# The fourth and fifth half-size products of a pair change places

## The chip, the cores and the metric

The kernel runs on one core of a Trainium2 chip. The metric is the device time of one execution in microseconds (us). A trace of one profiled execution stands beside the times. In it PE is TensorE's matmuls and PEld its weight loads, DVE is VectorE, ACT is ScalarE, POOL is GpSimd, SP is SyncE, which here only issues transfers; a name with a q is an engine's instruction queue issuing something.

## The reference

One layer of a state-space mixer over a sequence of 512 tokens with width 2048, all in float32:

```python
def reference(x, ...):                     # x: (1, 512, 2048)
    hn = rmsnorm(x, ln_g)
    proj = hn @ w_in                       # 2048 x 10304: z 4096 | x, B, C 6144 | dt 64
    xbc = silu(causal_depthwise_conv(xbc, conv_w, conv_b))
    dt = softplus(dt + dt_bias)
    y = ssd_chunked_scan(xs * dt, dt * a, bm, cm) + d_skip * xs    # 64 heads of 64, state 128
    y = rmsnorm(y * silu(z), norm_g)
    x = x + y @ w_out                      # 4096 x 2048
    return rmsnorm(x, final_g)
```

## The kernel before

**Precision.** A float32 operand is split into a high part (a cast to fp32r by ScalarE, line 87) and a low part (the difference, by VectorE, line 88). A product then takes three matmuls: high by high, high by low, low by high.

**Tiles.** The 80 tiles of 128 columns of the input projection are worked off in twos: a tile of x with one of z (32 of these), a tile of B with one of C (8). The first four twos are multiplied plainly. The other 36 go through `pair`, which uses a fast scheme with seven half-size products in place of eight. The weights of the two tiles, each in two halves of the contraction, are the blocks R11, R12 (first half of the contraction, first and second tile), R21, R22 (second half). Out of them come sums: T1 = R11 + R12, T2 = T1 + R22, T3 = R12 + R22, T4 = T2 + R21. (Signs are taken up by the forms of the activations, which are made ahead.) The output projection uses the same scheme in `opair`, in two groups of four pairs, between plain stretches.

**One pair of the input projection.** Each product is 24 matmuls of 128 x 128 by 256 (8 blocks of the contraction by 3). There are three accumulators in PSUM: S (half of one of two banks that take turns), R (one bank, used by every pair) and A (a bank). With a pair ahead of it, a pair runs, in TensorE's order:

1. R11 into S, then ScalarE copies S to A (line 651)
2. T1 into R, then ScalarE copies R out to `sn[:, 1]` (line 656)
3. T4 of the pair before into that pair's A
4. R22, on top of T1, into R
5. T2, on top of R11, into S, then ScalarE copies S out to `sn[:, 0]` (line 670) and VectorE adds R to it (line 671)
6. R21 into A
7. T3, on top of R11 and T2, into S, from which lines 675 and 676 read

The first pair has no pair ahead of it; it starts with T1, then R11, and lets its third place free.

**Preparing the weights.** Each of the R blocks is a transfer of 512 KB. `q_load` issues it on SP (line 81) into the raw buffers `ra` (three, for R11), `rb` (one, for R12) and `rc` (two, for R22 and R21 in turn). `q_fetch` lets POOL add a block to a raw buffer in place by an accumulating transfer (line 598: T1 and T3). `q_add` adds in place on VectorE (line 604: T2 on top of T1's raw piece, and T4 on top of T2's). `q_split` makes the high and low parts: R11 has a pair of buffers of its own, `h1h` and `h1l`, and all the others take turns in three pairs, `hi` and `lo`.

**Order.** The program order of TensorE, SP and POOL is the order in which the kernel is written. Work around the products is entered as events at a step: a pair is 28 steps long, a product four, and `run(step)` emits what is due. `q_events` enters a pair's loads, sums and splits by an offset to the pair's first step b. ScalarE and VectorE are ordered by a planner when the kernel is built: program order is their priority, `urgent()` raises it, and the planner's model of durations decides when something counts as ready. Between the products the scan's work for the tiles done before (transposes, decay, state, gate) is emitted in the same way. With each pair of B and C comes the convolution of these two tiles.

In the output projection S and R take turns in six banks, and VectorE reads them into the accumulator in SBUF: line 881 reads R after T1, line 893 R after R22, line 896 S after T2, line 898 A, line 903 S after T3; line 902 is ScalarE's copy for the last product. Its splits are urgent.

Of the kernel before, what the change touches and what calls it, by code (L numbers as in the profile page):

```python
# [13 lines left out]
ALU = mybir.AluOpType  # L14
# [6 lines left out]
KT = DM // P  # L21
# [13 lines left out]
def mamba_layer(ctx: ExitStack, tc: tile.TileContext, d: dict, out: bass.AP):  # L35
    nc = tc.nc
    V, S, T, Q = nc.vector, nc.scalar, nc.tensor, nc.gpsimd
# [3 lines left out]
    urgent = tc.high_priority  # L41
# [67 lines left out]
    NPL = 8  # L109
# [6 lines left out]
    quads = seq[NPL // 2:]  # L116
    tile_of = {"z": 0, "x": 32, "B": 64, "C": 72}
    QS = 28
# [21 lines left out]
    base = [END]  # L140
# [77 lines left out]
    q0, q1 = slice(0, 4), slice(4, 8)  # L218
# [203 lines left out]
    def g_c(g):  # L422
        gr[g]["C"] = conv_silu(40 + g, "bc")
        gr[g]["Cs"] = split(gr[g]["C"][:, LH:L], [P, LH], "cst", 2)
# [182 lines left out]
    qs = {}  # L607
    oquads = [blk for blk in blocks if type(blk) is tuple]

    def q_events(n, b, last, e=0, t1=0):  # L610
        for o, f, a in ((-38 - e, q_load, ("R11", 0, 0, "ra")), (-23 - e, q_split, ("R11", True)),
                        (-23 - e, q_fetch, ("T1", "R11", 0, 1)), (-3 - e // 2 - t1, q_split, ("T1",)),
                        (-12 - e // 2, q_load, ("R22", 1, 1, "rc")), (1 - e // 2, q_add, ("T2", "T1", "R22")),
                        (5, q_split, ("R22",)), (9, q_split, ("T2",)),
                        (-8, q_load, ("R21", 1, 0, "rc")), (12, q_add, ("T4", "T2", "R21")),
                        (13, q_split, ("R21",)),
                        (-7, q_load, ("R12", 0, 1, "rb")), (-7, q_fetch, ("T3", "R12", 1, 1)),
                        (17, q_split, ("T3",)), (23 if last else 29, q_split, ("T4",))):
            add(b + o, f, n, *a)
# [7 lines left out]
    def product(ps, w, f, first, step):  # L627

        for k in range(KH):
            if k % 2 == 0:  # L630
                run(step + k // 2)
            hi, lo = w()
            ah, al = operand(f, k)
            T.matmul(ps, hi[:, k, :], ah, start=first and k == 0, stop=False, skip_group_check=True)  # L634
            T.matmul(ps, hi[:, k, :], al, start=False, stop=False, skip_group_check=True)  # L635
            T.matmul(ps, lo[:, k, :], ah, start=False, stop=k == KH - 1, skip_group_check=True)  # L636

    def pair(n, prev):

        b = NPL * KT + n * QS  # L640
        (kp, ip), (kq, iq) = quads[n]
        s_, r_ = ps_s.tile([P, L], F32, name="S")[:, lo_], ps_q.tile([P, LH], F32, name="R")
        sn = sp.tile([P, 2, LH], F32, name="sn")
        zq = xr[:, 3:L + 3] if kq == "C" else sp.tile([P, L], F32, name="z", bufs=2)
        W = lambda f: lambda: qs[n, f]
        A = ps_mm.tile([P, L], F32, name="mm")

        def first(step):
            product(s_, W("R11"), 11, True, step)
            with urgent():  # L650
                S.copy(out=A[:, lo_], in_=s_)

        def second(step):
            product(r_, W("T1"), 1, True, step)
            with urgent():
                S.copy(out=sn[:, 1, :], in_=r_)  # L656

        if prev:
            first(b)
            second(b + 4)  # L660
            prev(b + 8)
        else:
            second(b)
            first(b + 4)
            for i in range(8, 12):
                run(b + i)
        product(r_, W("R22"), 4, False, b + 12)
        product(s_, W("T2"), 2, False, b + 16)
        with urgent():
            S.copy(out=sn[:, 0, :], in_=s_)  # L670
            V.tensor_tensor(out=zq[:, lo_], in0=r_, in1=sn[:, 0, :], op=ALU.add)
        product(A[:, lo_], W("R21"), 12, False, b + 20)
        product(s_, W("T3"), 3, False, b + 24)
        with urgent():
            V.tensor_tensor(out=zq[:, hi_], in0=s_, in1=sn[:, 1, :], op=ALU.add)
            S.copy(out=A[:, hi_], in_=s_)  # L676
        if kq == "C":
            V.scalar_tensor_tensor(out=zq, in0=zq, scalar=-1.0, in1=rbc, op0=ALU.mult, op1=ALU.mult)
            g_c(iq)
        else:  # L680
            V.tensor_tensor(out=zq, in0=zq, in1=rbc, op=ALU.mult)
            S.activation(zq, zq, AF.Silu, scale=-1.0)
            un[iq]["z"] = zq

        def last(step):
            product(A[:, hi_], W("T4"), 22, False, step)
            with urgent():
                normed(A)
            (g_b if kp == "B" else u_x)(ip)
            qs.pop(n)  # L690
        return last
# [4 lines left out]
    def add(step, f, *a):  # L696
        ev.setdefault(step, []).append((f, a))
# [8 lines left out]
        for o, f in zip(w, (u_load, u_decay, u_xt, u_state, u_yd, u_yo)):  # L706
            add(at["x", u] + o, f, u)
    for n in range(len(quads)):
        q_events(n, NPL * KT + n * QS, n == len(quads) - 1, 0 if n else 14)
    for i in range(4):  # L710
        add(49 + 7 * i, x_forms, i // 2, i % 2)
        add(114 + 4 * i, x_form3, i)
# [1 line left out]
    def run(step):  # L714
        for f, a in ev.pop(step, ()):
            f(*a)
# [80 lines left out]
    prev = None  # L797
    for n in range(len(quads)):
        prev = pair(n, prev)


    step = END
# [46 lines left out]
    def oproduct(ps, i, w, f, first, step):  # L849

        yh, yl = yform[i, f]
        for t in range(2):
            tt = slice(t * P, (t + 1) * P)
            for k in range(4):
                if k % 2 == 0:
                    run(step + 2 * t + k // 2)
                hi, lo = w()
                st, en = first and t == 0 and k == 0, k == 3
                T.matmul(ps[:, t, :], yh[:, k, tt], hi[:, k, :], start=st, stop=False, skip_group_check=True)  # L859
                T.matmul(ps[:, t, :], yl[:, k, tt], hi[:, k, :], start=False, stop=False, skip_group_check=True)  # L860
                T.matmul(ps[:, t, :], yh[:, k, tt], lo[:, k, :], start=False, stop=en, skip_group_check=True)  # L861

    def opair(i, s, b, prev):

        n = len(quads) + 4 * i + s
        s_, r_ = [ps_o.tile([P, 2, LH], F32, name="mm") for _ in range(2)]
        W = lambda f: lambda: qs[n, f]
        c = [slice(s * L + h * LH, s * L + h * LH + LH) for h in range(2)]
        p0, p1 = acc[:, 0:2, c[0]], acc[:, 2:4, c[0]]
        q0, q1 = acc[:, 0:2, c[1]], acc[:, 2:4, c[1]]  # L870
        A0 = ps_mm.tile([P, 2, LH], F32, name="mm")

        def first(step):
            oproduct(s_, i, W("R11"), 11, True, step)
            with urgent():
                S.copy(out=A0, in_=s_)

        def second(step):
            oproduct(r_, i, W("T1"), 1, True, step)
            with urgent():  # L880
                V.tensor_tensor(out=q1, in0=q1, in1=r_, op=ALU.subtract)

        if prev:
            first(b)
            second(b + 4)
            prev(b + 8)
        else:
            second(b)
            first(b + 4)
            for k in range(8, 12):  # L890
                run(b + k)
        oproduct(r_, i, W("R22"), 4, False, b + 12)
        V.tensor_tensor(out=q0, in0=q0, in1=r_, op=ALU.subtract)
        oproduct(s_, i, W("T2"), 2, False, b + 16)
        with urgent():
            V.tensor_tensor(out=q0, in0=q0, in1=s_, op=ALU.subtract)
        oproduct(A0, i, W("R21"), 12, False, b + 20)
        V.tensor_tensor(out=p0, in0=p0, in1=A0, op=ALU.add)
        oproduct(s_, i, W("T3"), 3, False, b + 24)
        A1 = ps_mm.tile([P, 2, LH], F32, name="mm")  # L900
        with urgent():
            S.copy(out=A1, in_=s_)
        V.tensor_tensor(out=q1, in0=q1, in1=s_, op=ALU.subtract)

        def last(step):
            oproduct(A1, i, W("T4"), 22, False, step)
            V.tensor_tensor(out=p1, in0=p1, in1=A1, op=ALU.add)
            qs.pop(n)
        return last
# [38 lines left out]
    m = 0  # L948
    for i, blk in enumerate(blocks):
        if type(blk) is tuple:  # L950
            for s in range(4):
                q_events(len(quads) + 4 * m + s, base[i] + s * QS, s == 3, 0, 3 if s == 0 else 0)
            for j in range(2):
                add(base[i] - ((50, 32), (54, 32))[m][j], y_fetch, m, j)
                add(base[i] - ((39, 24), (47, 24))[m][j], y_forms, m, j)
            m += 1
# [21 lines left out]
    prev = None  # L978
    step += 4
    phx.close()  # L980
    op = ctx.enter_context(tc.tile_pool(name="op", bufs=1, side="right"))
# [4 lines left out]
    m = 0  # L986
    for kb, blk in enumerate(blocks[:-1]):
        if type(blk) is tuple:
            assert step == base[kb], (step, base[kb])
            for s in range(4):  # L990
                prev = opair(m, s, step, prev)
# [4 lines left out]
        for s, pairs in blk:  # L996
            ps = [None] * NC
            for p in pairs:
# [4 lines left out]
                for t in range(NC):  # L1003
# [15 lines left out]
                    if prev and t > 0:  # L1019
                        prev(step)  # L1020
                        step += 4
                        prev = None
# [13 lines left out]
    for t in range(NC):  # L1036
        ss = fp.tile([P, 4], F32, name="ss", bufs=2)
        for s in range(4):
            ps = ps_o.tile([P, L], F32, name="mm")
            for i in range(2):  # L1040
# [6 lines left out]
                            op=ALU.mult)  # L1047
# [6 lines left out]
        n = 2 if t < NC - 1 else 4  # L1054
# [43 lines left out]
```

## Time and profile before

| | |
|---|---|
| time, median of 3 runs | 1301.98 us (1300.03 to 1308.32) |
| the profiled execution | 1302.64 us |
| its span, first to last instruction | 1300.9 us |
| mean granted TensorE clock | 0.993 |
| PE busy | 1250.4 us, 96%, 9932 matmuls |
| PEld busy | 1188.6 us, 91% |
| DVE busy | 1082.3 us, 83% |
| ACT busy | 827.6 us, 64% |
| DMA | 225.90 MB, mean 174 GB/s |

The 36 pairs of the input projection fill the span from about 120 to 945 us, the output projection with its plain stretches what follows. A row of the time line gives the start, the duration, engine, line, operation, output and inputs, and in brackets the engine's idle time before it with what ended it. Rows of waits give who waited for whom, the total, how often, and the longest. Weight loads overlap matmuls, and matmuls overlap one another, so a busy engine isn't one at its peak.

### The profile page before, as it was taken

The numbers are of one execution on the slowest core, as the hardware profiler recorded it, in microseconds if no ns is written. First come the engines' busy times: TensorE is split into PE (matmuls) and PEld (weight loads), VectorE is DVE, ScalarE is ACT, GpSimd is POOL, SyncE is SP. The second block draws the span as 40 slices with busy tenths as digits, with TensorE's granted clock in tenths as the row PEclk, the third lists the DMA queues.
The fourth block names the chain that finished last, engine by engine and source line by source line (L and its number), as shares of the span: only waits on it lengthen the run. The fifth ranks groups of instructions, "written<-read, shape, count | busy, mean of one in ns | idle before, by whom it ended". The sixth has DMA issues, their size and how long they took to land.

```text
span 1300.9 us, 24461 instructions
## 1 busy us (share of the span) xinstructions
PE 1250.4 (96%) x9932; PEld 1188.6 (91%) x9932; DVE 1082.3 (83%) x1449; ACT 827.6 (64%) x1357; POOL 77.7 (6%) x99
## 2 busy tenths in 40 slices
PE   8989999999999999999999999999899899999997
PEld 7989899999999999999999999999888799789885
DVE  5796888989988998988899899889856887878865
ACT  7667667578666857766785777668655444534523
POOL 0000001010100101010000101010000000001000
PEclk9999999999999999999999999999999999999998
DMA  9546657575685667567566656756636677658612
GB/s 357 174 143 184 173 146 173 154 193 141 188 207 156 165 168 182 146 184 209 156 158 192 158 158 180 218 143 154 185 107 205 201 181 221 197 130 220 201 42 98
DMA packets 70194, 225.90 MB, mean 174 GB/s; under 512 B 8384, under 2 KB 12800, under 8 KB 69952
## 3 DMA queue, kind: packets, MB, share of 16 engines
q1 hardware_dynamic: 56688, 176.34, 40.5%
q0 software_dynamic: 12672, 46.14, 21.4%
q8 instruction: 78, 1.28, 0.4%
q10 hardware_dynamic: 720, 1.84, 0.4%
q14 instruction: 36, 0.29, 0.1%
HBM read 211.52 MB, written 12.78 MB: 172 GB/s over the span
## 4 chain that ended last, share of the span: by engine, by line
PE 59%; DVE 15%; DMA 11%; ACT 8%; issue 6%; SPq 0%; POOL 0%; DVEq 0%; ACTq 0%; POOLq 0%
PE S L636 5%; PE S L634 5%; PE S L635 5%; PE mm L859 3%; PE mm L634 3%; PE mm L860 3%; PE mm L915 3%; PE mm L861 3%; PE mm L917 3%; PE mm L916 3%; PE R L634 3%; PE R L635 3%; PE R L636 3%; DMA ra<-in_wi 3%; DVE lo L88 3%
## 5 line engine op out<-in xcount | busy, mean ns | idle before, releaser
L88 DVE TENSOR_TENSOR lo<-ra,hi 128x1024 fp32r<-128x1024 f32 x150 | 180.7, 1220 | 55.9 <-ACT hi L87 55.7
L87 ACT CAST hi<-ra 128x1024 fp32r<-128x1024 f32 x150 | 154.7, 1047 | 85.7 <-PE mm L860 19.7
L634 PE MATMUL mm<-xh,hi 128*128 128x256 f32 x576 | 163.8, 284 | 0.0
L634 PE MATMUL R<-s,hi 128*128 128x256 f32 x576 | 160.7, 279 | 2.6 <-ACT sn L656 2.6
L87 ACT CAST hi<-rc 128x1024 fp32r<-128x1024 f32 x94 | 98.4, 1047 | 101.0 <-DMA rc<-in_wi 58.5
L636 PE MATMUL mm<-xh,lo 128*128 128x256 f32 x576 | 160.7, 279 | 0.3 <-DVE lo L88 0.3
L635 PE MATMUL mm<-xl,hi 128*128 128x256 f32 x576 | 160.6, 279 | 0.0
L636 PE MATMUL R<-s,lo 128*128 128x256 f32 x576 | 160.2, 278 | 0.0
L635 PE MATMUL R<-s,hi 128*128 128x256 f32 x576 | 160.2, 278 | 0.0
L604 DVE TENSOR_TENSOR ra<-ra,rc 128x1024 f32<-128x1024 f32 x88 | 107.4, 1220 | 33.9 <-DMA rc<-in_wi 33.5
L88 DVE TENSOR_TENSOR lo<-rc,hi 128x1024 fp32r<-128x1024 f32 x94 | 114.5, 1218 | 0.9 <-ACT hi L87 0.8
L634 PEld LDWEIGHTS mm<-xh,hi 128*128 128x128 f32 x576 | 108.4, 188 | 5.1 <-issue 5.0
L634 PEld LDWEIGHTS R<-s,hi 128*128 128x128 f32 x576 | 108.2, 188 | 3.4 <-ACT sn L656 3.4
L636 PEld LDWEIGHTS mm<-xh,lo 128*128 128x128 f32 x576 | 109.3, 190 | 0.5 <-DVE lo L88 0.5
L636 PEld LDWEIGHTS R<-s,lo 128*128 128x128 f32 x576 | 109.0, 189 | 0.0
L635 PEld LDWEIGHTS mm<-xl,hi 128*128 128x128 f32 x576 | 108.5, 188 | 0.1
L635 PEld LDWEIGHTS R<-s,hi 128*128 128x128 f32 x576 | 108.2, 188 | 0.0
L634 PE MATMUL S<-xh,hi 128*128 128x256 f32 x288 | 81.4, 282 | 9.8 <-ACT sn L670 7.5
L636 PE MATMUL S<-xh,lo 128*128 128x256 f32 x288 | 82.2, 285 | 4.3 <-DVE lo L88 4.3
L634 PE MATMUL S<-xh,h1h 128*128 128x256 f32 x288 | 83.3, 289 | 1.0 <-ACT mm L676 1.0
L635 PE MATMUL S<-xl,hi 128*128 128x256 f32 x288 | 80.3, 279 | 0.7 <-DVE xl L578 0.7
L635 PE MATMUL S<-xl,h1h 128*128 128x256 f32 x288 | 80.6, 280 | 0.0
(452 smaller groups left out, 3929.2 us busy)
## 6 DMA issues: line engine op xcount, KB each, us to landing
rc<-in_wi SPq DMA_DIRECT2D x76, 512.0 KB, 5.3
ra<-in_wi SPq DMA_DIRECT2D x42, 512.0 KB, 6.1
rb<-in_wi SPq DMA_DIRECT2D x40, 512.0 KB, 7.5
ra<-in_wi POOLq DMA_DIRECT2D x36, 512.0 KB, 7.7
rb<-in_wi POOLq DMA_DIRECT2D x36, 512.0 KB, 6.4
csb<-cscr SPq DMA_DIRECT2D x32, 512.0 KB, 8.7
ra<-in_wo SPq DMA_DIRECT2D x26, 512.0 KB, 5.2
yscr<-xs SPq DMA_DIRECT2D x32, 256.0 KB, 2.7
```

The costliest lines, as they stand in the source:

```text
L87: S.copy(out=hi, in_=raw)
L88: V.tensor_tensor(out=lo, in0=raw, in1=hi, op=ALU.subtract)
L604: V.tensor_tensor(out=raw, in0=raw, in1=qs[n][other], op=ALU.add)
L634: T.matmul(ps, hi[:, k, :], ah, start=first and k == 0, stop=False, skip_group_check=True)
L635: T.matmul(ps, hi[:, k, :], al, start=False, stop=False, skip_group_check=True)
L636: T.matmul(ps, lo[:, k, :], ah, start=False, stop=k == KH - 1, skip_group_check=True)
L859: T.matmul(ps[:, t, :], yh[:, k, tt], hi[:, k, :], start=st, stop=False, skip_group_check=True)
L860: T.matmul(ps[:, t, :], yl[:, k, tt], hi[:, k, :], start=False, stop=False, skip_group_check=True)
L861: T.matmul(ps[:, t, :], yh[:, k, tt], lo[:, k, :], start=False, stop=en, skip_group_check=True)
L915: T.matmul(ps, yh, hi, start=first and k == 0, stop=False)
L916: T.matmul(ps, yh, lo, start=False, stop=False)
L917: T.matmul(ps, yl, hi, start=False, stop=last and k == 1)
```

## The change

For every pair that has a pair ahead of it, in both projections, the fourth and fifth products swap: T2 into S comes ahead of R22 into R. With them go what is attached to each: ScalarE's copy of S out to `sn[:, 0]` in `pair`, and VectorE's reads at lines 893 and 896 in `opair`. VectorE's add at line 671 stays behind both. The events of the two splits change offsets: T2's goes from 9 to 5, R22's from 5 to 9. The first pair of the input projection, and the first of each group of the output projection (`lone`), keep the old order and offsets.

```diff
-    def q_events(n, b, last, e=0, t1=0):
+    def q_events(n, b, last, e=0, t1=0, lone=False):
...
-                        (5, q_split, ("R22",)), (9, q_split, ("T2",)),
+                        *(((5, q_split, ("R22",)), (9, q_split, ("T2",))) if lone else
+                          ((5, q_split, ("T2",)), (9, q_split, ("R22",)))),
...
-        product(r_, W("R22"), 4, False, b + 12)
-        product(s_, W("T2"), 2, False, b + 16)
-        with urgent():
-            S.copy(out=sn[:, 0, :], in_=s_)
+        def third(step):
+            product(r_, W("R22"), 4, False, step)
+
+        def fourth(step):
+            product(s_, W("T2"), 2, False, step)
+            with urgent():
+                S.copy(out=sn[:, 0, :], in_=s_)
+
+        for f, step in zip((fourth, third) if prev else (third, fourth), (b + 12, b + 16)):
+            f(step)
+        with urgent():
             V.tensor_tensor(out=zq[:, lo_], in0=r_, in1=sn[:, 0, :], op=ALU.add)
...
-        oproduct(r_, i, W("R22"), 4, False, b + 12)
-        V.tensor_tensor(out=q0, in0=q0, in1=r_, op=ALU.subtract)
-        oproduct(s_, i, W("T2"), 2, False, b + 16)
-        with urgent():
-            V.tensor_tensor(out=q0, in0=q0, in1=s_, op=ALU.subtract)
+        def third(step):
+            oproduct(r_, i, W("R22"), 4, False, step)
+            V.tensor_tensor(out=q0, in0=q0, in1=r_, op=ALU.subtract)
+
+        def fourth(step):
+            oproduct(s_, i, W("T2"), 2, False, step)
+            with urgent():
+                V.tensor_tensor(out=q0, in0=q0, in1=s_, op=ALU.subtract)
+
+        for f, at_ in zip((fourth, third) if prev else (third, fourth), (b + 12, b + 16)):
+            f(at_)
...
-        q_events(n, NPL * KT + n * QS, n == len(quads) - 1, 0 if n else 14)
+        q_events(n, NPL * KT + n * QS, n == len(quads) - 1, 0 if n else 14, lone=not n)
...
-                q_events(len(quads) + 4 * m + s, base[i] + s * QS, s == 3, 0, 3 if s == 0 else 0)
+                q_events(len(quads) + 4 * m + s, base[i] + s * QS, s == 3, 0, 3 if s == 0 else 0, s == 0)
```

## The prediction

> **What bounds the kernel now.** I read the totals first, then the waits of TensorE, then one pair of output tiles on each engine in order of time. In what follows the seven half-size products of a steady pair stand in slots: 1 is R11 into S, 2 is T1 into R, 3 is T4 of the pair before into A, 4 is R22 into R, 5 is T2 into S, 6 is R21 into A, 7 is T3 into S. The change swaps what is done in slots 4 and 5. Pairs are counted from 0 to 35.
>
> The view of stretches, over the 36 pairs (its columns: length, then busy time of PE, weight loads, DVE, ACT, POOL):
>
> ```profile
> 120.00:945.00 825.00, 804.34 (x6896) 780.01 (x6896) 726.12 (x936) 578.28 (x990) 60.30 (x70) 1.00 0.66 171
> ```
>
> TensorE is busy 804.34 of 825.00 us at a granted clock of 1.00. So no reordering can win more here than the 20.7 us in which it stands still, and VectorE with 726.12 is the next to press. What those still moments are, by the view of waits for the same stretch (total, times, longest):
>
> ```profile
> PE S L634 <- ACT sn L670: 7.5, 7, 1.8
> PE S L636 <- DVE lo L88: 4.3, 6, 1.4
> PE R L634 <- ACT sn L656: 2.6, 4, 1.1
> ```
>
> The first row is slot 7: T3 may not add onto S before ScalarE has copied the sum of slots 1 and 5 out of it (L670). The third is slot 4: R22 may not add onto R before T1's result is copied out (L656). The second is a weight split that ends late; where I followed it, it is T3's low part, in slot 7 again. Only these rows can be reached by an exchange of slots 4 and 5.
>
> Why the copy at L670 is late, in pair 21, ScalarE:
>
> ```profile
> 613.14 1.06 ACT L87 CAST hi<-rb 128x1024 fp32r<-128x1024 f32 x1 [1.74 <-DMA rb<-in_wi]
> 614.98 1.04 ACT L87 CAST hi<-ra 128x1024 fp32r<-128x1024 f32 x1 [0.78 <-DMA ra<-in_wi]
> 615.93 0.36 ACT L670 COPY sn<-S 128x256 f32<-128x256 f32 x1
> ```
>
> It is not late by its own work of 0.36. It stands on ScalarE behind two casts, T3's and the next pair's T1's, each of which waited for a transfer. TensorE then shows
>
> ```profile
> 616.34 0.39 PE L634 MATMUL S<-xh,hi 128*128 128x256 f32 x1 [1.60 <-ACT sn L670]
> 616.57 0.28 PE L635 MATMUL S<-xl,hi 128*128 128x256 f32 x1
> 616.69 0.28 PE L636 MATMUL S<-xh,lo 128*128 128x256 f32 x1
> ```
>
> **The change, part by part.** The number of instructions and bytes stays the same. What moves is which wait ends when.
>
> *The copy of S out (gain).* S is complete after slot 4 and not after slot 5, and T3 still starts in slot 7. The slots of this pair start at
>
> ```profile
> 606.42 0.28 PE L634 MATMUL R<-s,hi 128*128 128x256 f32 x1
> ```
> ```profile
> 609.14 0.28 PE L634 MATMUL S<-s,hi 128*128 128x256 f32 x1
> ```
>
> so the copy gets 2.72 us more, and the longest wait of the row was 1.8. Its 7.5 us go, as long as ScalarE's order puts the copy where S is ready. Likewise R22 moves from slot 4 to slot 5, so the copy at L656 gets 2.72 us against a longest wait of 1.1: 2.6 us go. Together 10.1.
>
> *What is late next (given back).* After a relieved wait the next thing in the pair is T3's low part. In pair 21 VectorE has it at
>
> ```profile
> 614.36 1.22 DVE L88 TENSOR_TENSOR lo<-rb,hi 128x1024 fp32r<-128x1024 f32 x1
> ```
>
> to 615.58. Its first reader is the third matmul, 616.69, which without the 1.60 would come at 615.09: 0.5 comes back. The same subtraction (the third matmul stands 0.35 behind the first) for the three other long ones, pairs 11, 25 and 31:
>
> ```profile
> 389.11 1.22 DVE L88 TENSOR_TENSOR lo<-rb,hi 128x1024 fp32r<-128x1024 f32 x1
> ```
> ```profile
> 391.00 0.38 PE L634 MATMUL S<-xh,hi 128*128 128x256 f32 x1 [1.84 <-ACT sn L670]
> ```
> ```profile
> 706.97 1.22 DVE L88 TENSOR_TENSOR lo<-rb,hi 128x1024 fp32r<-128x1024 f32 x1
> ```
> ```profile
> 708.83 0.39 PE L634 MATMUL S<-xh,hi 128*128 128x256 f32 x1 [1.32 <-ACT sn L670]
> ```
> ```profile
> 840.65 1.22 DVE L88 TENSOR_TENSOR lo<-rb,hi 128x1024 fp32r<-128x1024 f32 x1
> ```
> ```profile
> 842.76 0.39 PE L634 MATMUL S<-xh,hi 128*128 128x256 f32 x1 [1.38 <-ACT sn L670]
> ```
>
> 390.33 against 391.00+0.35-1.84 = 389.51 gives back 0.8; 708.19 against 707.86 gives back 0.3; 841.87 against 841.73 gives back 0.1. With pair 21 that is 1.7. The three other waits of the row hold 1.36 together; I take them whole. The waits at L656 fare worse. In pair 16 the view of waits from 494 to 505 says
>
> ```profile
> PE R L634 <- ACT sn L656: 1.1, 1, 1.1
> PE S L636 <- DVE lo L88: 0.7, 1, 0.7
> ```
>
> Both are in one pair, so TensorE freed of the first runs into the second 1.1 us sooner and waits as much longer. Two more of the four waits stand in such a pair (6 and 26) and the fourth in pair 11, already short by T3. So I count all 2.6 as handed on. From these rows: 10.1 - 1.7 - 2.6 = 5.8.
>
> *T2's chain (what the swap asks for).* T2 is a sum that VectorE makes from T1 and R22 (L604), then ScalarE's cast, then VectorE's low part. In pair 21:
>
> ```profile
> 597.98 1.23 DVE L604 TENSOR_TENSOR ra<-ra,rc 128x1024 f32<-128x1024 f32 x1 [1.13 <-DMA rc<-in_wi]
> ```
> ```profile
> 601.32 1.22 DVE L88 TENSOR_TENSOR lo<-rc,hi 128x1024 fp32r<-128x1024 f32 x1
> 603.04 1.23 DVE L88 TENSOR_TENSOR h1l<-ra,h1h 128x1024 fp32r<-128x1024 f32 x1 [0.51 <-ACT h1h L87]
> 606.89 1.22 DVE L88 TENSOR_TENSOR lo<-ra,hi 128x1024 fp32r<-128x1024 f32 x1 [2.63 <-ACT hi L87]
> 608.03 0.68 DVE L398 TENSOR_TENSOR xr<-mm,rbc 128x512 f32<-128x512 f32 x1
> 608.63 1.22 DVE L604 TENSOR_TENSOR ra<-ra,rc 128x1024 f32<-128x1024 f32 x1
> ```
>
> R22's low part is done at 602.54, 4.1 before slot 4's third matmul (606.42+0.23). T2's is done at 608.11, 1.3 before slot 5's (609.14+0.23). The three high/low buffers rotate in the order of the split events, so with the events exchanged T2 takes R22's buffer and place. From the sum's end, 599.21, a cast (1.05) and a low part (1.22) need until 601.5, the place at 601.32 or a little later. So slot 4 keeps some 4 us of cover and costs nothing. Without that cover, with T2 at its present 608.11, slot 4 would wait 1.5 (the second rival). R22 takes T2's place and buffer, with the 1.3 of cover there.
>
> *The sum for T4* (608.63) waits for T2's raw piece to be split. With T2 early, VectorE can make it in the 2.63 idle before 606.89, since R21 is there; that takes 1.22 out of the full stretch before T3's low part. Between nothing and the 4.3 us of the row "S L636" I take 1, near the low end, because in pair 21 the cast of T3 waits for its transfer whatever VectorE does.
>
> *Transfers.* R22's raw piece is let go one place later. On SP the next pair's R22 load is issued right behind R22's low part (602.54), and the load of the next R11 but one behind it:
>
> ```profile
> 602.56 0.33 SPq L81 DMA_DIRECT2D rc<-in_wi  x1
> 602.94 0.43 SPq L81 DMA_DIRECT2D ra<-in_wi  x1
> 611.47 0.33 SPq L81 DMA_DIRECT2D rc<-in_wi  x1
> ```
>
> Both go to about 608.1; the load behind them on SP, at 611.47, is not moved. The first is needed by the next pair's sum, a pair's length after 597.98 (825.00 over 36 is 22.9 us, so about 620.9), and lands a median 5.3 us after issue:
>
> ```profile
> rc<-in_wi SPq DMA_DIRECT2D x76, 512.0 KB, 5.3
> ```
>
> so at 613.4, with over 7 us of cover. POOL's queue keeps its order.
>
> *Output stage.* There S and R are read out by VectorE. The first pair of each group keeps the old order; in the others the exchange gives L881 and L896 one slot more. From 1160 to 1200, and from 1215 to 1230, the waits are
>
> ```profile
> PE mm L859 <- DVE acc L881: 0.8, 2, 0.5
> ```
> ```profile
> PE mm L859 <- ACT mm L902: 1.1, 1, 1.1
> PE mm L859 <- DVE acc L896: 0.6, 1, 0.6
> ```
>
> The 0.8 go. The 0.6 are followed by the 1.1 at L902, so they are handed on. Gain 0.8.
>
> *Pace of the matmuls.* Two stretches of 9 us with nothing but products, both without a wait and at clock 1.00:
>
> ```profile
> 362.00:371.00 9.00, 9.00 (x79) 9.00 (x78) 7.89 (x12) 4.46 (x6) 0.00 (x0) 1.00 0.67 130
> 404.00:413.00 9.00, 9.00 (x82) 9.00 (x81) 8.15 (x12) 8.96 (x18) 0.00 (x0) 1.00 0.14 27
> ```
>
> 79 against 82 matmuls: TensorE has a slower pace, about 0.1 us for a product of 24. What switches it the trace does not say. If a wait ends a slow stretch, taking the wait away lets it run on; ten products more would cost 1 us. The end of the scale is all 252 products of the pairs, 25 us; fifty of them either way are -5 to +5, which I keep for the range, and take -1.
>
> **Sum.** 5.8 + 1 + 0.8 - 1 = 6.6 us off the profiled 1302.64 (a span of 1300.9 and 1.7 around it): 1296.0. The median shown is 0.7 lower than the profiled time, so 1295.4; I give 1296.
>
> **Rivals.**
>
> *Handed on whole, 1302.* Every wait was on an in-order queue, and the planner orders ScalarE and VectorE anew. If T3's low part comes later by what TensorE gains, nothing is left. For it: three of the four L656 waits. Against it: in the four long waits of L670 the rows above leave 4.4 of 6.1 us free.
>
> *T2 late, 1305.* The place: slot 4's third matmul behind T2's low part. It decides when that low part ends over 5.1 us after it could (601.5 against the 606.65 of pair 21); at its present time it does. Pairs 6, 11, 16, 21, 26 and 31, the second after a B and C pair, are alike in having little cover there; at 1.5 each they lose 9, less the 6.6: 2.4 more than before, 1305. A planner that leaves T2's cast behind the decay work on ScalarE would do it. Against: the cast could run from 599.21, and the low part behind it now starts at 606.89.
>
> *T3 early too, 1288.* T3's accumulating transfer, issued by POOL, was
>
> ```profile
> 602.52 0.86 POOL L598 DMA_DIRECT2D rb<-in_wi  x1 [17.98 <-DMA rb<-in_wi]
> ```
>
> and its cast began at 613.14, on its landing: 10.6 us, beside the two loads of 602.56 and 602.94. The same transfer's median is 6.4:
>
> ```profile
> rb<-in_wi POOLq DMA_DIRECT2D x36, 512.0 KB, 6.4
> ```
>
> If those loads move to 608 and T3 lands some us sooner, and the T4 sum moves as above, all three rows go with the output's 0.8: 7.5 + 4.3 + 2.6 + 0.8 = 15.2, 1287.4 from the profiled time; with 1 back for the pace, 1288. The Trainium skill ("DMA: Bandwidth & Descriptors", section "Queues, rings and completion order") says that each DMA engine takes turns between its queues packet by packet; by that rule the moved loads leave T3's transfer more turns. The trace agrees as far as 10.6 against 6.4 goes; no row shows the transfer without the loads in this same pair.
>
> **Chances.** Forecast (1293 to 1299) 0.45, handed on (1299.5 to 1302.5) 0.22, T3 early (below 1291) 0.17, T2 late or a worse order of an engine (above 1303) 0.16. The range is 1288 to 1304: it leaves out about 0.1 on either side. One per cent, about what a measurement of this kernel can tell from no change, is 13 us: below 1289 it is faster, 0.13; above 1315 slower, for which each pair would have to lose 0.4 us, 0.05; within 0.82.
>
> **What would show it.** The rows "S L634 <- ACT sn L670" and "R L634 <- ACT sn L656" should be gone or below 1 us; "S L636 <- DVE lo" should hold 4 to 8 us; no row "S L636" or "S L634" should be waiting for T2 at the start of slot 4; the load of the next R22 in pair 21 should come 5 us later against slot 1; T3's cast tells by its time after POOL's issue whether the third rival is at work. It would be wrong if the planner's new order puts a copy or T3's split behind a cast that waits for a transfer, or if the slow pace fills more of the span.

## The result, and the profile after

The changed kernel takes 1294.88 us, the median of 20 runs (1290.52 to 1299.11); the kernel before takes 1303.99 us beside it, also a median of 20. One of those 20 took 4718.66 us and is left out of the ratio; the others lie between 1295.3 and 1308.32. The ratio is 0.9936 with a 95% interval of [0.9922, 0.995], a gain of 9.1 us between the medians. Its profiled execution took 1295.7 us with a span of 1294.0. In the changed kernel the matmuls of the pairs stand at L635 to L637, the copies of S and R at L674 and L657, the output's matmuls at L867 to L869, its two subtractions at L907 (S, was L896) and L889 (R's, first product) and its copy for T4 at L916 (was L902).

The view of stretches, same columns as before:

```profile
120.00:945.00 825.00, 814.29 (x6975) 790.65 (x6974) 738.27 (x949) 587.55 (x1007) 60.36 (x71) 1.00 0.67 173
```

In the same 825 us TensorE now gets through 6975 matmuls, where it was 6896. The 79 more, at 825/6975 = 0.118 us each, are 9.3 us of work done earlier. The waits of TensorE over the whole span (total, times, longest):

```profile
PE S L637 <- DVE lo L88: 5.6, 9, 1.5
...
PE mm L867 <- DVE acc L907: 2.5, 1, 2.5
PE mm L869 <- DVE lo L88: 1.8, 2, 1.4
PE mm L867 <- ACT mm L916: 1.7, 1, 1.7
PE mm L867 <- DVE acc L889: 1.7, 1, 1.7
...
PE mm L930 <- DVE lo L88: 1.2, 1, 1.2
```

No row for the copies is left: the 7.5 and the 2.6 us are gone. Of the three rows shown before, 14.4 us in all, the 5.6 of the late low part are what remains. The waits for L916 and L930 belong to the output; the first was 1.1 and the second isn't among the rows of before.

Where the time went can be read from the first starts of two groups of matmuls, the first product of the pairs and the first product of the output (columns: duration least, median, most in ns; then the first and last start). Before, then after:

```profile
L634 PE MATMUL R<-s,hi x576: 276/276/388, 120.9 to 927.8; 128*128 128x256 f32 x192
```
```profile
L859 PE MATMUL mm<-hi,f1h x64: 276/276/281, 1017.2 to 1206.7; 128*128 128x256 f32 x64
```
```profile
L635 PE MATMUL R<-s,hi x576: 276/276/281, 121.3 to 923.3; 128*128 128x256 f32 x192
```
```profile
L867 PE MATMUL mm<-hi,f1h x64: 276/281/281, 1005.3 to 1198.4; 128*128 128x256 f32 x64
```

From the first pair to the first output product it was 1017.2 - 120.9 = 896.3 us and is 884.0. From there to the end of the span it was 1300.9 - 1017.2 = 283.7 and is 288.7. So **in these two profiles the pairs are 12.3 us shorter and the output is 5.0 longer**. The same two lengths in us, from the same rows of all profiled runs (the edits are told below):

| kernel | pairs | output |
|---|---|---|
| before | 896.3 | 283.7 |
| full change, three profiles | 884.0, 882.4, 881.9 | 288.7, 287.4, 286.8 |
| change in the input pairs alone, two profiles | 884.0, 884.4 | 282.4, 284.9 |
| change in the output alone | 898.0 | 287.5 |
| output: products swapped, splits in the old order | 883.0 | 285.4 |
| full change, but the last pair of each output group in the old order | 884.3 | 286.5 |
| products swapped alone, in both projections | 893.3 | 284.7 |
| splits exchanged alone, in both projections | 897.9 | 290.1 |
| R12's load earlier, in the kernel before | 895.0 | 292.1 |
| R12's load earlier, with the change in the input pairs | 903.2 | 291.9 |
| T3's split ahead, with the change in the input pairs | 897.7 | 283.8 |

In the rows without a further edit the pattern is this: the pairs gain 12 to 14 us where both halves of the change are in them, 3.0 with the products alone, and lose 1.6 with the splits alone. The output takes 286.5 to 290.1 us where its splits are exchanged, and 282.4 to 285.4 where they aren't.

A few us of such a length can be pace. Of the output's 1824 matmuls, 157 start 116 to 120 ns after the one ahead in the profile of before; 662, 274 and 680 do in the full change, and 1292 with the change in the output alone; most others start 112 to 115 ns apart. At 5 ns each this is 0.6 to 5.7 us more than before, the last of them more than the whole difference of that profile (3.8). So against the one profile of before the lengths don't tell what the order costs the output. Against the change in the input pairs alone they do: its two profiles have 749 and 774 slow starts, more than the full change, and are shorter all the same, with 5.9 and 6.9 us of stops of TensorE in the output against 8.2 to 10.0. That the output's new order costs time rests on the medians further down.

### The profile page after: what moved, and what is told of

The parts are those of the page before. It is cut to its first block, busy times and chain, and to the rows that moved or that the text cites. A ratio compares the mean times of both kernels' runs of the same rounds, so it can differ in the third digit from the quotient of the medians.

```text
span 1294.0 us, 24519 instructions
## 1 busy us (share of the span) xinstructions
PE 1252.1 (97%) x9932; PEld 1192.9 (92%) x9932; DVE 1084.3 (84%) x1449; ACT 826.6 (64%) x1357; POOL 77.5 (6%) x99
## 4 chain that ended last, share of the span: by engine, by line
PE 74%; DVE 11%; DMA 7%; issue 4%; ACT 3%; SPq 0%; POOL 0%; DVEq 0%; ACTq 0%; POOLq 0%
PE S L637 7%; PE S L635 7%; PE S L636 7%; PE mm L635 5%; PE mm L636 4%; PE R L635 4%; PE mm L637 4%; PE R L636 4%; PE R L637 4%; DVE lo L88 3%; PE mm L929 3%; PE mm L931 3%; PE mm L930 3%; PE yd L502 2%; PE mm L867 2%
## 5 line engine op out<-in xcount | busy, mean ns | idle before, releaser
L635 PE MATMUL mm<-xh,hi 128*128 128x256 f32 x576 | 163.6, 284 | 0.0
L637 PE MATMUL mm<-xh,lo 128*128 128x256 f32 x576 | 160.6, 279 | 0.6 <-DVE lo L88 0.6
L637 PE MATMUL R<-s,lo 128*128 128x256 f32 x576 | 160.3, 278 | 0.1
L635 PE MATMUL R<-s,hi 128*128 128x256 f32 x576 | 160.2, 278 | 0.0
L635 PEld LDWEIGHTS mm<-xh,hi 128*128 128x128 f32 x576 | 108.1, 188 | 5.2 <-issue 5.0
L637 PEld LDWEIGHTS mm<-xh,lo 128*128 128x128 f32 x576 | 109.2, 190 | 0.8 <-DVE lo L88 0.8
L637 PEld LDWEIGHTS R<-s,lo 128*128 128x128 f32 x576 | 109.1, 189 | 0.3 <-DVE lo L88 0.3
L635 PEld LDWEIGHTS R<-s,hi 128*128 128x128 f32 x576 | 108.2, 188 | 0.0
L637 PE MATMUL S<-xh,lo 128*128 128x256 f32 x288 | 83.5, 290 | 5.6 <-DVE lo L88 5.6
L635 PE MATMUL S<-xh,h1h 128*128 128x256 f32 x288 | 83.4, 290 | 1.0 <-DVE xr L398 1.0
L635 PE MATMUL S<-xh,hi 128*128 128x256 f32 x288 | 81.3, 282 | 2.2 <-ACT xh L577 1.3
```

## The experiments

All of them were timed beside the kernel before; each ratio carries its 95% interval.

### The full change again, and its two halves

The full change was timed twice more.

> The changed kernel once more, beside the others on one chip. My theory (the copies of S and R out of PSUM get a slot more, and the loads of the next R22 and R11 no longer share the engines with T3's transfer) expects about 8 us less than before, and in the profile no wait for either copy again. The view of waits should show 4 to 7 us for T3's low part as in the first profile of it. If the pace of the matmuls belongs to the program, the first group of the output projection is slow again (about 86 us from its first product to its last); if it belongs to the execution, it may be 82 us.

> The full change as it is, on the same chip as the kernel with the old order of splits in the output: 1293 to 1296, a ratio of 0.992 to 0.994 to the kernel before.

Measured: 1293.4 us, 0.992 [0.9895, 0.9946], and 1294.97 us, 0.994 [0.9919, 0.9961]. No copy's wait came back. T3's low part was waited for 2.9 and 4.5 us, once below the 4 to 7 expected. In the first profile 604 starts of the output's first group stood at the slower pace, in these two 58 and 624, so the pace isn't fixed by the program.

**The products alone.** The fourth and fifth products swap, the two splits keep their order.

```diff
-                        *(((5, q_split, ("R22",)), (9, q_split, ("T2",))) if lone else
-                          ((5, q_split, ("T2",)), (9, q_split, ("R22",)))),
+                        (5, q_split, ("R22",)), (9, q_split, ("T2",)),
```

> The products change places as in the change, the two split events keep the old offsets, so T2's split follows R22's and takes the buffer that T1 leaves. My theory: T2 comes where it came before, 1.5 to 1.8 us too late for slot 4 in pairs 6, 11, 16, 21, 26 and 31; 9 to 11 us of waits for T2's cast or low part at slot 4 in place of the copies' waits; time 1302 to 1306, at any rate 6 us or more over the full change. Rival: the order of the products alone brings the gain and the planner moves T2's split up by itself: within 2 us of the full change.

Measured: 1302.19 us, 0.9977 [0.9961, 0.9993]: 2 of the 9 us, as the theory had it. The rows for the copies are gone, though T3's transfer in the pairs 6, 11, ... 31 still took 8.0 to 9.2 us from issue to landing, about as before (8.5 to 10.5). So the slot alone is enough for the copies. In their place stand, in the waits of this kernel:

```profile
PE S L636 <- DVE lo L88: 6.9, 14, 0.9
PE S L634 <- ACT hi L87: 2.9, 4, 1.3
```

They look like the waits for T3. The time line of pair 16 says otherwise:

```profile
495.32 0.28 PE L636 MATMUL mm<-xh,lo 128*128 128x256 f32 x1
495.97 0.39 PE L634 MATMUL S<-s,hi 128*128 128x256 f32 x1 [0.37 <-ACT hi L87]
496.20 0.28 PE L635 MATMUL S<-s,hi 128*128 128x256 f32 x1
497.23 0.38 PE L636 MATMUL S<-s,lo 128*128 128x256 f32 x1 [0.75 <-DVE lo L88]
497.45 0.29 PE L634 MATMUL S<-s,hi 128*128 128x256 f32 x1
```

This is S fed from a sum form (s), not from xh: it is T2 at the start of slot 4. VectorE had its low part where T2's stood before:

```profile
495.95 1.22 DVE L88 TENSOR_TENSOR lo<-ra,hi 128x1024 fp32r<-128x1024 f32 x1 [3.13 <-ACT hi L87]
```

It ends at 497.17, and the third matmul starts at 497.23. The same wait stands in pairs 6, 11, 16, 21, 26 and 31, with 0.5, 1.1, 1.1, 0.75, 1.6 and 0.75 us: 5.8 in all, of 9 to 11 expected. The remaining 4.0 us of the two rows stand in slot 7.

The five rows of TensorE show one thing more. Undisturbed, a matmul starts 0.12 us after the one before it while that one still runs (0.28). Around the wait of 0.37 the starts are 495.97 - 495.32 = 0.65 apart and the next 0.23. That is (0.65 - 0.12) + (0.23 - 0.12) = 0.64 lost where the row says 0.37. Over 194 waits of 0.15 to 3 us in the fourteen profiles, with matmuls of one shape on both sides, the difference is 0.27 us in the median and 0.24 to 0.27 in nine of ten: **a wait costs nearly 0.3 us more than its row**.

**The splits alone.** T2 is split ahead of R22, the products keep their old order.

```diff
-        for f, step in zip((fourth, third) if prev else (third, fourth), (b + 12, b + 16)):
+        for f, step in zip((third, fourth), (b + 12, b + 16)):
...
-        for f, at_ in zip((fourth, third) if prev else (third, fourth), (b + 12, b + 16)):
+        for f, at_ in zip((third, fourth), (b + 12, b + 16)):
```

> The two splits change places, T2's sum ahead of R22, but the products keep the old order: R22's weights are used in the fourth slot, T2's in the fifth. The loads behind R22's low part go late as in the full change, so T3's accumulating transfers of the pairs after a B or C block take 5.4 to 5.7 us. Theory (the slot between S's copy and S's next product removes the copies' waits, the transfers do not): the copies' waits stay at 5 to 9 us in all, R22's low part is now late for the fourth slot in some of the pairs, by 0 to 2 us each, and the time is 1305 to 1315. Rival (the gain comes from the moved loads): S's wait for the copy goes below 3 us and the time to 1297 to 1301.

Measured: 1308.62 us, 1.003 [1.0006, 1.0053]. The time is inside the theory's range, its reason isn't what happened: the copies' rows are gone here too. The waits in the pairs' stretch now begin with

```profile
PE R L637 <- DVE lo L88: 10.1, 12, 2.9
PE R L635 <- ACT hi L87: 1.5, 2, 0.8
```

R22's low part is late for slot 4, in the very pairs in which slot 7 waited before and their neighbours. TensorE stops earlier in the pair, and ScalarE has caught up by slot 7. So this run doesn't say whether the shorter transfers of T3 (5.4 to 5.7 us here) would have freed the copies by themselves.

By the table most of what the splits alone lose stands in the output; the pairs lose 1.6 us. In the pairs each half makes late just what the other half makes early, and together they gain what neither does.

### T3's transfer

**R12's load six steps earlier** on SP's queue, ahead of the loads that share the DMA engines with T3's accumulating transfer: once in the kernel before, once with the change in the input pairs alone (the output's pairs get the earlier load as well).

```diff
-                        (-7, q_load, ("R12", 0, 1, "rb")), (-7, q_fetch, ("T3", "R12", 1, 1)),
+                        (-13, q_load, ("R12", 0, 1, "rb")), (-7, q_fetch, ("T3", "R12", 1, 1)),
```

> The kernel before, with one event moved: each pair's load of R12 is issued on SP ahead of the loads of R22 and of the next R11, not behind them. R12's buffer comes free only with T3's low part, so the two loads behind it are held until then and don't run beside T3's and T1's accumulating transfers in pairs 6, 11, 16, 21, 26 and 31. Products and splits stay in the old order. If the gain came from the slot more for the copies (theory), the waits for the copy out of S stay mostly, above 4 us, and the time is within 3 us of before. If it came from the moved loads (rival), T3's transfer takes 5.5 to 6.5 us there and not 9 to 10.5, ScalarE's casts no longer hold up the copy, its waits fall below 2.5 us, and 4 us or more are won.

Measured: 1310.2 us, 1.0053 [1.0033, 1.0073]. T3's transfer did not get shorter (median 8.4 us where it was 6.4), so the run missed its aim and doesn't decide between the theory and the rival. The time is 6 us above before, where the theory allowed 3; by the table the output is 8.4 us longer, and the pairs are 1.3 shorter. The copies' waits stayed:

```profile
PE S L634 <- ACT sn L670: 5.4, 6, 1.0
PE R L634 <- ACT sn L656: 3.5, 4, 1.9
```

> The change in the 36 input pairs alone, with R12's load issued six steps earlier, ahead of the next loads on its queue, in all pairs. Nothing else is moved; the accumulating transfers of T3 then share the engines with the next loads again and take some 8.4 us instead of 5.5 us in the pairs after a B or C block. Theory (the short transfer is half of the gain: with the new order alone S waits for T3's low part instead of its copy): S's wait for the low part rises from 4.4 to 4.8 us to 7 to 10 us, no wait for S's copy comes back, and the time is 1294 to 1300. Rival (the new slot alone gives the gain): the wait stays under 5.5 us and the time at 1288 to 1291.

Measured: 1321.78 us, 1.0152 [1.0118, 1.0186], 31 us above the same kernel without the edit, far beyond the forecast. The waits rose as the theory said, and no copy's wait came back:

```profile
PE S L637 <- DVE lo L88: 11.7, 15, 2.0
...
PE S L635 <- ACT hi L87: 6.1, 8, 1.3
```

But the transfer isn't what holds them. In pair 21, POOL and ScalarE:

```profile
608.02 0.86 POOL L598 DMA_DIRECT2D rb<-in_wi  x1 [16.61 <-DVE z L689]
```
```profile
623.01 1.03 ACT L87 CAST hi<-rb 128x1024 fp32r<-128x1024 f32 x1
```

T3 landed 8.5 us after its issue, at 616.5, and its cast began 6.5 us later, behind the decay work of the pair's head, with no wait for a transfer in its row. That work is itself late. R12's load waits for its buffer (2.5 us on SP for a low part on VectorE ahead of pair 21), and on SP's queue everything behind it waits too: the load that the decay needs (`csb`) lands 7.6 us after the pair's first start, where it is 4.8 with the change in the input pairs alone (second profile). ScalarE's order is another as well, so the shares of the two aren't shown. By the table the pairs are 19 us longer than without the edit, and the output 7 to 10. The time can't be put down to the longer transfer, so this run leaves open whether the short transfer is half of the gain; no run took it alone away.

### Only the input pairs, only the output

```diff
-        for f, at_ in zip((fourth, third) if prev else (third, fourth), (b + 12, b + 16)):
+        for f, at_ in zip((third, fourth), (b + 12, b + 16)):
...
-                q_events(len(quads) + 4 * m + s, base[i] + s * QS, s == 3, 0, 3 if s == 0 else 0, s == 0)
+                q_events(len(quads) + 4 * m + s, base[i] + s * QS, s == 3, 0, 3 if s == 0 else 0, True)
```

> The change in the 36 pairs of the input projection alone; the output projection keeps the old order and offsets. My theory: nearly all of the gain, 7 to 9 us less than before, since the output's share was put at 0.8. Rival (the output projection's pace is set by the new order there): the output projection's first group goes back from 86 to 82 us, and the kernel is 2 to 5 us faster than the full change.

> The change in the 36 input pairs alone, once more, on the same chip as the kernel with the change in the output alone. Theory: 1288 to 1290, some 15 us under the unchanged kernel, of which the pairs' stage gives 10 to 12 us; the rest of the difference to the full change lies in the output. If the output's order costs nothing, the two differ by chance alone and this run stands at 1293 to 1296.

Measured: 1288.9 us, 0.9882 [0.9858, 0.9907], and 1290.6 us, 0.9892 [0.9868, 0.9915]. The first is 4.5 us below the full change beside it, the second 4.3 below that change's median of 20. The first theory's 7 to 9 us were too few, and its rival's time came, but not by the pace that it named: in the first repeat of the full change the first group ran at the faster one with the new order too. The mirror image, `zip((third, fourth), ...)` and `lone=True` in the input pairs alone:

> The output projection's eight pairs have the new order, the 36 input pairs the old one. Theory (the new order costs time at the end of the output's second group): the S copies' waits of the input pairs stay (L670-type 5 to 8 us, L656-type 2 to 4 us), and the time is 2 to 5 us over the unchanged kernel, some 1306 to 1309. By the prediction's term for the output (0.8 us gained) it is at or just under the unchanged kernel, 1302 to 1304. If the 4.5 us between the full change and the change in the input pairs alone were no property of the order, this kernel stands within 1 us of the unchanged one.

Measured: 1308.7 us, 1.0033 [1.0012, 1.0054], that is 1.6 to 7.0 us slower than the kernel before, as the theory had it; the copies' waits stayed (6.5 and 1.9 us). The two parts add up: 0.9887 on average for the one plus 0.0033 is 0.992, where the full change has 0.992 to 0.994.

The loss has a visible part at the end of the output's second group. ScalarE's waits for the last weights of Wo, which are cast into the buffers of the forms f2 and f4 as these come free; first the full change, then the change in the output alone:

```profile
ACT f2h L958 <- DMA ra<-in_wo: 4.1, 1, 4.1
```
```profile
ACT f2h L958 <- DMA ra<-in_wo: 3.9, 1, 3.9
```

With the change in the input pairs alone there is no such row. Behind these casts in ScalarE's queue stand the cast for T4's weights and the copy at L916, for which TensorE waits 1.7 us at one place in all four profiles of the full change and of the change in the output alone, and not at all in the two with the change in the input pairs alone (1.1 in the kernel before). From the last pair's T1 product to the end of the span it is 97.6 to 99.1 us in these four, 95.3 and 95.2 in these two, and 96.6 before.

These rows don't stand for the whole loss. With the splits exchanged alone there is no row for f2h, less than 0.1 us for L916 and an end of 94.8 us, and yet the output is the longest of all without a further edit (290.1). With the products swapped alone the row for f2h is 2.1 and the wait 1.5, and the output is among the shorter ones (284.7).

**Not in the last pair.** In `opair`, `if prev and s < 3`, and `s in (0, 3)` for `lone`, so that the last pair of each group keeps the old order:

> The full change except in the last pair of each of the output's two groups, which keeps the old order. Theory (the output's loss sits in the last pair of the second group, where the casts of the last output weights, waiting for their loads, stand ahead of the copy for the closing product): the waits for that copy (1.7 us) and for the low part just ahead of it (1.2 us) go, and the time is 1289 to 1292, within 1.5 us of the change in the input pairs alone and 3 to 5 us under the full change. Rival (the loss is spread over the output's other pairs, or is no loss): 1293 to 1296 as with the full change.

Measured: 1293.64 us, 0.9922 [0.9903, 0.9941]. The theory's time didn't come. Of its two waits the one for the low part is gone and the one for the copy halved, and the end is 96.9 us:

```profile
PE mm L867 <- ACT mm L916: 0.9, 1, 0.9
```

So the last pair's own order is at most a part of the loss. The interval, from five runs, overlaps that of the change in the input pairs alone, and where the remainder arises in the pairs ahead isn't shown.

**The products swapped in the output, the splits in their old order** (the full change in the input pairs):

```diff
-                q_events(len(quads) + 4 * m + s, base[i] + s * QS, s == 3, 0, 3 if s == 0 else 0, s == 0)
+                q_events(len(quads) + 4 * m + s, base[i] + s * QS, s == 3, 0, 3 if s == 0 else 0, True)
```

> The full change in the 36 input pairs; in the output's pairs the two products change places, but the two splits keep their old order, R22's ahead of T2's, so that the buffer of R22's weights comes free when it did before. Theory (the output's loss of 3 to 5 us comes from the splits: R22's raw weights are held longer, so the loads behind them and the casts of the last weights go late): 1288 to 1291, as with the change in the input pairs alone, and no 4 us gap on ScalarE before the cast of the last weights. Rival (the loss comes from the order of the products and of the sums on VectorE): 1293 to 1297.

Measured: 1289.37 us, 0.9898 [0.987, 0.9927]; the full change on the same chip was 5.6 us slower. The waits of TensorE for L916 and L930 are gone, and ScalarE's is

```profile
ACT f2h L958 <- DMA ra<-in_wo: 1.0, 1, 1.0
```

So in the output it is the order of the splits that costs; with the products swapped alone, too, the output (284.7) is as long as where it isn't changed (282.4 to 284.9). R22's raw weights are held one place longer, and the load that takes their buffer goes out behind R22's low part. SP, in the last pair of the full change and of this run:

```profile
1203.43 0.33 SPq L81 DMA_DIRECT2D rc<-in_wo  x1
```
```profile
1196.39 0.38 SPq L81 DMA_DIRECT2D rc<-in_wo  x1
```

The last pair of this run stands 3.0 us earlier (its T1 product at 1192.95 against 1196.03), so the load is 4 us earlier in the pair, and the loads of Wo behind it on SP follow. In the four profiles named above this load stands 7.0 to 8.5 us behind the T1 product, with the input pairs alone and in this run 3.4. The end of the span is 95.3 us behind the T1 product here. So 2 to 4 us of the loss are at the end, with the late loads ahead of them; that the loads cause all of it isn't shown, as the splits alone (load at 5.2, end 94.8) lose elsewhere.

### T3's split ahead of other work

The change in the input pairs alone, and in `q_split`:

```diff
-        with urgent() if n >= len(quads) else ExitStack():
+        with urgent() if n >= len(quads) or f == "T3" else ExitStack():
```

> The change in the 36 input pairs alone, and the split of T3's weights placed ahead of other ready work on ScalarE and VectorE. Theory (what is left of the late T3 is the order of ScalarE's and VectorE's work and no longer its transfer): the wait of S's product for the low part falls from 4.8 us to under 1.5, and the time to 1284 to 1287. Rival (the part is late because the engines' work ahead of it is needed as well): the wait moves to another product, and the time stays at 1288 to 1292.

Measured: 1308.06 us, 1.0026 [1.0006, 1.0047]. The rival's mechanism holds, at a far higher price than it named, and the waits come in the pairs, which lose all that the change had won there: S's wait for the low part fell to 0.6, and these came instead:

```profile
PE mm L635 <- ACT mm L684: 6.3, 4, 2.0
...
PE tr L473 <- ACT xs L394: 4.0, 6, 2.0
PE R L637 <- DVE lo L88: 4.0, 5, 1.2
```

## Why the prediction was right, and where its steps were off

The median was put at 1296 and is 1294.9. The mechanism in the pairs was right: the copies' waits go, T2 comes in time, and T3's low part is what is left. That the number is so near is in part luck. The sum won 6.6 us from a profile of 1302.64, and 9.1 us between the medians were measured. The pairs gained 12 to 14 us where the terms for them make 5.8 (5.8 + 1 - 1), the output lost some 4 where 0.8 was to be won, and the two errors work against each other.

- **The copies' waits, 10.1 us.** Right: both rows are gone in all three profiles of the full change, and with the products swapped alone.
- **T2's chain, no cost.** Right. In pair 21 of the changed kernel:

```profile
597.75 1.22 DVE L88 TENSOR_TENSOR lo<-ra,hi 128x1024 fp32r<-128x1024 f32 x1
599.01 1.23 DVE L604 TENSOR_TENSOR ra<-ra,rc 128x1024 f32<-128x1024 f32 x1
```
```profile
602.90 0.28 PE L637 MATMUL S<-s,lo 128*128 128x256 f32 x1
```

  T2's low part ends at 598.97, 3.9 us ahead of its reader; some 4 were forecast. The rival "T2 late" is what the products alone did: it named those six pairs and 1.5 us for each, and 0.5 to 1.6 was measured. It needed T2 to stay at its old place, and the exchanged splits took it from there.
- **The sum for T4.** Right that it moves: the second row above stands 4.5 us after the start of the pair's slot 1 (594.51), where it was 10.4 (608.63 against 598.26).
- **Given back, 4.3 of the 10.1, and 1 gained by that sum.** Too pessimistic: of the 14.4 us in the three rows 7.6 should have stayed, and 5.6, 2.9 and 4.5 did in the three profiles. In the first of them pair 6 has no wait at all, where the L656 wait was to be handed on, and pairs 25 and 31 have none. Pair 16 is nearly as forecast, 1.54 for its low part (1.1 + 0.7 before). Pair 21 is worse than forecast: it waits 1.33 where 0.5 was to come back. There VectorE's order is what is left:

```profile
608.62 1.75 DVE L461 TENSOR_TENSOR m<-m,cbm 128x1536 f32<-128x1536 f32 x1
610.29 0.75 DVE L391 SCALAR_TENSOR_TENSOR xs<-xr,par,xs 128x512 f32<-128x512 f32 x1
610.95 0.42 DVE L679 TENSOR_TENSOR z<-R,sn 128x256 f32<-128x256 f32 x1
611.28 1.22 DVE L88 TENSOR_TENSOR lo<-rb,hi 128x1024 fp32r<-128x1024 f32 x1
```

- **Left out: the rest of a wait.** The pairs' stretch gained 12.3, 13.9 and 14.4 us from three rows that fell by 8.8, 11.5 and 9.9. Of the rest, seven or eight fewer waits, each nearly 0.3 us dearer than its row, make some 2. The bound of 20.7 us for the pairs leaves this out as well. And the output's first plain product, which stands in this stretch and whose waits weren't looked at, waits 1.5 to 1.7 us less. In the first two profiles this is all but 0.3 us, with the pace below counted; in the third, some 2.5 us more stay unexplained. The product's rows before, and the one that remains:

```profile
PE S L915 <- ACT hi L87: 1.2, 1, 1.2
...
PE S L916 <- DVE lo L88: 0.9, 1, 0.9
```
```profile
PE S L930 <- DVE lo L88: 0.5, 1, 0.5
```

- **Transfers, no cost.** Right for the pairs. The next R22's load in pair 21 goes out 10.4 us after slot 1 (604.96 against 594.51) where it was 4.3 later; 5 more were forecast, 6.1 came, and nothing waits for it. For the output the same step fails: "R22's raw piece is let go one place later" was followed on SP in the input pairs only.
- **The output, +0.8.** Wrong in sign: by the medians the output's new order costs 4 to 6 us (4.5 and 4.3 between the full change and the input pairs alone, 4.3 for the output alone, 5.6 against the splits in the old order). The step looked at the two subtractions that get one slot more, and not at the loads and casts behind the longer-held buffer, where the last weights of Wo have no cover.
- **Pace, -1.** About right. Of the 6048 matmuls of the pairs, 2702 started 116 to 120 ns after the one ahead before, and 2805, 3012 and 3075 after; the others mostly 112 to 115. At 5 ns each these are 0.5 to 1.9 us.
- **T3 early too.** Its mechanism came, its gain can't be told apart. The issue in pair 21, and the cast:

```profile
599.12 0.86 POOL L598 DMA_DIRECT2D rb<-in_wi  x1 [18.23 <-DVE lo L88]
```
```profile
608.12 0.35 ACT L674 COPY sn<-S 128x256 f32<-128x256 f32 x1
608.37 1.06 ACT L87 CAST hi<-rb 128x1024 fp32r<-128x1024 f32 x1
```

  The transfer landed at 604.7, 5.6 us after the issue and ahead of the moved loads; it took 10.5 beside them. But the cast comes 3.6 us after the landing, and the low part behind VectorE's other work. The Trainium skill's rule that was cited there ("DMA: Bandwidth & Descriptors", section "Queues, rings and completion order"), that a DMA engine takes turns between its queues, would leave T3 more turns with the loads moved away: in the six pairs 5.4 to 5.6 us against 8.5 to 10.5 agree with it.
- **Handed on whole.** Not so with the full change. But the run with T3's split ahead shows that what is left at T3 isn't to be had by moving that split ahead alone.

## What to carry to other kernels

When two steps change places, move what prepares them too, and check both halves by themselves: in the stretch of the input pairs the products alone brought 3 us, the splits alone lost 1.6, and both together brought 12 to 14. Then do the sum again for each stage that shares the edit, down to the loads that wait for the buffers: the same exchange of splits that pays in the input pairs costs 4 to 6 us in the output, where swapping the products alone is free. The version to keep is the change in the input pairs, with or without the swapped products of the output (1288.9 to 1290.6 us).

## What the runs showed of the hardware

A stop of TensorE costs more than the idle time in its row, by nearly 0.3 us here. The row counts from the end of the matmul ahead, 0.28 us after that one's start, while an undisturbed matmul would have started after 0.12; that is 0.16. The successor then starts 0.23 after the first matmul behind the stop and not 0.12; that is 0.11.

Matmuls of one shape at a granted clock of 1.00 start either 113 or 118 ns apart, in spells of dozens to hundreds. The program alone doesn't set which it is: the output's first group ran at 118 in two profiles of the full change and at 113 in the third. A slower spell often ends at a wait: over the fourteen profiles, of 152 waits above 0.3 us with a slow spell in the 20 starts ahead, 94 have the faster pace in the 20 starts behind, 14 the slow one, and 44 a mix. What switches the pace isn't shown. Without a wait the slow pace can run on: with the change in the input pairs alone the output's second group stayed at it for nearly all of its starts, in both profiles. So a wait taken away can return less than it seems where a slow spell then runs on, and returns nearly 0.3 us more where none does.
